# Rotary embedding on one core: each 2 MB slab as one stretch of DRAM, the cos and sin tables loaded in two halves

## The chip, the cores and the metric

The kernel runs on one core of a Trainium2 chip. The metric is device microseconds of one execution, median of the runs. The profile shows a second figure, the span: the time from the first to the last instruction that it recorded. In a run's own record the time is about 1.8 us above its span, for instance 165.31 us of time at a span of 163.5 us.

An execution more than 1.5% above the fastest of the same kernel counts as slow and is left out of every comparison; the others are fast.

The names in the profile: DVE is VectorE, ACT is ScalarE, POOL is GpSimd, PE is TensorE (PEld its weight loads), SP is SyncE; a q behind the name marks the issuing of DMA transfers. SBUF and PSUM are the two on-chip memories that hold the kernel's tiles, the blocks of 128 partitions (rows) that it names. A packet is one piece of a DMA transfer.

## The reference

```python
x:   [8, 2048, 8, 64] float32      # batch, position, head, d_head
cos, sin: [2048, 32] float32       # position, half of d_head

x1, x2 = x[..., :32], x[..., 32:]
out1 = x1 * cos - x2 * sin
out2 = x1 * sin + x2 * cos
out  = concatenate([out1, out2], axis=-1)
```

33.55 MB are read and 33.55 MB are written. The tables are 0.26 MB each.

## The kernel before

The 2048 positions of one batch are spread over 128 partitions, 16 neighbouring positions a partition: 32 KB of each partition's row. A slab is half of that, 8 positions a partition, 16 KB in each of 128 partitions, 2 MB. There are 16 slabs, first the eight batches with `l = 0`, then the eight with `l = 1`. Nine SBUF buffers hold slabs.

```python
    xv = x.rearrange("b (q r) h d -> b q (r h d)", q=P)
    ov = out.rearrange("b (q r) h d -> b q (r h d)", q=P)
    cos_src = cos.rearrange("(q r) d -> q r d", q=P)
    # ... sin_src alike
    cos_ps = tab_pool.tile([P, R, Dh], f32, tag="cp")      # PSUM, 128 x 512 fp32
    sin_ps = tab_pool.tile([P, R, Dh], f32, tag="sp")      # PSUM, 128 x 512 fp32
    # ... t1: PSUM, one buffer of 128 x 2048 fp32; o: PSUM, two of 128 x 512
    # ... t2: SBUF, three buffers

    def load(i):                                    # queue of SyncE
        b, l = slabs[i]
        xt = xpool.tile([P, SLAB], f32, tag="xt", name=f"xt{i}")
        for lo, n in spans(cuts(i)):                # slab 0 in two, the others whole
            nc.sync.dma_start(out=xt[:, lo : lo + n],
                              in_=xv[b, :, l * SLAB + lo : l * SLAB + lo + n])
            if i == 0 and lo == 0:
                nc.sync.dma_start(out=cos_sb, in_=cos_src)
                nc.sync.dma_start(out=sin_sb, in_=sin_src)
    for i in range(NBUF):                           # NBUF = 9
        load(i)

    # ... eye
    nc.scalar.mul(nsin, sin_sb, -1.0)
    nc.scalar.mul(neye, eye, -1.0)
    nc.vector.tensor_copy(cos_ps, cos_sb)
    nc.scalar.copy(sin_ps, sin_sb)
```

The arithmetic is mostly of kind "A": GpSimd writes x times sin into t2 in two instructions, VectorE multiplies x by cos from PSUM into t1, and then adds t1 and t2 back into the slab.

```python
            for u, tab in ((1, sin_sb), (0, nsin)):
                nc.gpsimd.tensor_mul(out=t2u[:, :, u, :]..., in0=xu[:, :, 1 - u, :]...,
                                     in1=rep(tab[:, r0 : r0 + nr, :], H))
        keep(nc.vector.tensor_mul(out=t1..., in0=xk, in1=rep(cos_ps[:, r0 : r0 + nr, :], 2 * H)))
        if kind == "A":
            keep(nc.vector.tensor_add(out=xt, in0=t1, in1=t2))
```

Slabs 5 and 10 use kinds "B" and "C": TensorE does the sum, and ScalarE copies it out of PSUM. ScalarE also issues the stores, two slabs behind, in its program order. So the stores of slab 3 and later stand behind ScalarE's copies for slab 5, and those of slab 8 and later behind its copies for slab 10. The load into a buffer waits for the store that empties it.

Of the kernel before, what the change touches and what calls it, by code (L numbers as in the profile page):

```python
# [10 lines left out]
def kernel(  # L11
# [7 lines left out]
    nc = tc.nc  # L19
# [6 lines left out]
    P = 128  # L26
# [3 lines left out]
    SL = 8  # L30
    n_half = R // SL
    SLAB = SL * HD
# [1 line left out]
    NBUF = 9  # L34
    C = 512

    xv = x.rearrange("b (q r) h d -> b q (r h d)", q=P)
    ov = out.rearrange("b (q r) h d -> b q (r h d)", q=P)
    cos_src = cos.rearrange("(q r) d -> q r d", q=P)
    sin_src = sin.rearrange("(q r) d -> q r d", q=P)  # L40

    const_pool = ctx.enter_context(tc.tile_pool(name="const", bufs=1))
    tab_pool = ctx.enter_context(tc.tile_pool(name="tab", bufs=1, space=PSUM))
# [6 lines left out]
    cos_sb = const_pool.tile([P, R, Dh], f32, tag="cb")  # L50
    sin_sb = const_pool.tile([P, R, Dh], f32, tag="sb")
    nsin = const_pool.tile([P, R, Dh], f32, tag="ns")
    eye = const_pool.tile([P, P], f32, tag="eye")
    neye = const_pool.tile([P, P], f32, tag="neye")
    cos_ps = tab_pool.tile([P, R, Dh], f32, tag="cp")
    sin_ps = tab_pool.tile([P, R, Dh], f32, tag="sp")
# [5 lines left out]
    def cuts(i):  # L62
        return [UNIT, UNIT] if i == 0 else [SLAB]
# [8 lines left out]
    def spans(sizes):  # L72
        lo = 0
        for n in sizes:
            yield lo, n
            lo += n

    def load(i):
        b, l = slabs[i]
        xt = xpool.tile([P, SLAB], f32, tag="xt", name=f"xt{i}")  # L80
        for lo, n in spans(cuts(i)):
            nc.sync.dma_start(
                out=xt[:, lo : lo + n],
                in_=xv[b, :, l * SLAB + lo : l * SLAB + lo + n],
            )
            if i == 0 and lo == 0:
                nc.sync.dma_start(out=cos_sb, in_=cos_src)
                nc.sync.dma_start(out=sin_sb, in_=sin_src)
        xts[i] = xt

    for i in range(NBUF):
        load(i)

    nc.gpsimd.memset(eye, 0.0)  # L94
    nc.gpsimd.affine_select(
        out=eye,
        in_=eye,
# [3 lines left out]
        pattern=[[-1, P]],  # L101
        channel_multiplier=1,
    )
    nc.scalar.mul(nsin, sin_sb, -1.0)  # L104
    nc.scalar.mul(neye, eye, -1.0)
    nc.vector.tensor_copy(cos_ps, cos_sb)  # L106
    nc.scalar.copy(sin_ps, sin_sb)  # L107

    def rep(a, n):
        return dataclasses.replace(a, ap=[a.ap[0][:], a.ap[1][:], [0, n], a.ap[-1][:]])  # L110
# [67 lines left out]
    def store(i, lo, n):  # L178
        b, l = slabs[i]
        keep(  # L180
            nc.scalar.dma_start(
                out=ov[b, :, l * SLAB + lo : l * SLAB + lo + n],
                in_=xts[i][:, lo : lo + n],
            )
        )

    for i in range(last + 1):
        if i == last:
            for k in range(i - LAG, i):
                store(k, 0, SLAB)  # L190
        for lo, n in spans(pieces(i)):
            rotate(i, lo, n)
            if i == last and lo == 0:
                store(i, 0, UNIT)
        if i == last:
            store(i, UNIT, UNIT)
        if LAG <= i < last:
            store(i - LAG, 0, SLAB)
        if i > LAG and i - LAG - 1 + NBUF <= last:
            load(i - LAG - 1 + NBUF)  # L200
# [30 lines left out]
```

## Time and profile before

| | before |
|---|---|
| time, median of 4 runs | 164.97 us |
| span of the profiled run | 163.5 us |
| VectorE busy / GpSimd busy | 142.8 / 138.8 us |
| DMA, two data queues, share of 16 engines' span | 49.8% + 48.6% |
| first multiply on VectorE | 6.90 us |
| first store issued | 19.25 us |

These are lines of the page's parts 2, 3 and 5. In part 2 a digit is the busy share of one fortieth of the span, in tenths. In part 5 the columns are line, engine, operation, tiles and shapes, count, then busy time and mean ns, then the idle time before and what ended most of it.

```profile
DVE  0439999999999999999999999999999999999900
POOL 1299999999999999699999999984999999995000
DMA  5999999999999999999999999999999999999995
...
q1 hardware_dynamic: 2736, 34.08, 49.8%
q10 hardware_dynamic: 2448, 33.56, 48.6%
...
L142 DVE TENSOR_TENSOR t<-xt,cos_ps 128x2048 f32<-128x2048 f32 (+1 forms) x34 | 73.5, 2168 | 1.0
...
L106 DVE COPY cos_ps<-cos_sb 128x512 f32<-128x512 f32 x1 | 0.7, 696 | 6.2 <-DMA cos_sb<-in_cos_dram 6.2
```

The DMA engines are full in every slice but the first and the last; 98.4% of 163.5 us is 160.9 us of work for each of the 16. VectorE (DVE) is almost as full. Two resources are thus near their limit. VectorE starts as soon as cos has been loaded and copied.

The timeline of the start, with start and length in us, engine, line and operation, and in brackets the idle time before it with its releaser:

```profile
6.17 0.70 DVE L106 COPY cos_ps<-cos_sb 128x512 f32<-128x512 f32 x1 [6.17 <-DMA cos_sb<-in_cos_dram]
...
6.90 1.23 DVE L142 TENSOR_TENSOR t<-xt,cos_ps 128x1024 f32<-128x1024 f32 x1
...
7.57 0.58 ACT L107 COPY sin_ps<-sin_sb 128x512 f32<-128x512 f32 x1
...
19.25 0.38 ACTq L181 DMA_DIRECT2D out_dram<-xt  x1
```

ScalarE's view (ACT) later on: after its last copy for slab 10 it issues the nine stores that are left.

```profile
121.02 0.59 ACT L156 COPY xt<-o 128x512 f32<-128x512 f32 x1 [1.13 <-PE o L155]
121.08 34.80 ACTq L181 DMA_DIRECT2D out_dram<-xt  x9
```

VectorE's last instruction of this run:

```profile
154.28 1.23 DVE L149 TENSOR_TENSOR xt<-t,t 128x1024 f32<-128x1024 f32 x1
```

In the trace's record of DMA packets a 16 KB packet took 611 ns in the median, for loads and for stores.

### The profile page before, as it was taken

What the parts mean: (1) busy time and instruction counts of PE and PEld (TensorE: products, weight loads), DVE (VectorE), ACT (ScalarE), POOL (GpSimd) and SP (SyncE); (2) the same over time, 40 slices, a digit from 0 to 9 for tenths busy, and PEclk for the clock granted to TensorE, in tenths of its full rate; (3) what the DMA queues carried; (4) which work ended last, traced back from release to release, by engine and by line L of the source; (5) the groups of instructions that cost most, each with busy time, mean ns of one, the idle gap of its engine ahead of it and who ended that gap; (6) DMA issues with size and microseconds to landing.
All of it is one profiled execution on the core that took longest, in us unless ns stands there. A gap on an engine that the chain in (4) does not pass through costs nothing. (4 is left out here: it accounts for less than half of the span.)

```text
span 163.5 us, 460 instructions
## 1 busy us (share of the span) xinstructions
PE 34.5 (21%) x64; PEld 13.8 (8%) x64; DVE 142.8 (87%) x67; ACT 12.0 (7%) x20; POOL 138.8 (85%) x70
## 2 busy tenths in 40 slices
PE   0000000000000049997000000699950000000000
PEld 0000000000000014442000000234410000000000
DVE  0439999999999999999999999999999999999900
ACT  3300000000000001233000000013320000000000
POOL 1299999999999999699999999984999999995000
PEclk9999999999999999999655555559996555555555
DMA  5999999999999999999999999999999999999995
GB/s 182 415 449 429 445 317 421 425 445 433 417 433 441 437 409 445 437 421 425 425 421 369 439 411 429 449 417 429 421 445 429 413 445 429 429 425 445 421 409 228
DMA packets 5186, 67.65 MB, mean 414 GB/s; under 512 B 576, under 2 KB 576, under 8 KB 832
## 3 DMA queue, kind: packets, MB, share of 16 engines
q1 hardware_dynamic: 2736, 34.08, 49.8%
q10 hardware_dynamic: 2448, 33.56, 48.6%
q14 instruction: 2, 0.02, 0.0%
HBM read 34.08 MB, written 33.55 MB: 414 GB/s over the span
## 5 line engine op out<-in xcount | busy, mean ns | idle before, releaser
L136 POOL TENSOR_TENSOR t<-xt,sin_sb 128x1024 f32<-128x1024 f32 (+1 forms) x32 | 70.4, 2201 | 10.3 <-DMA sin_sb<-in_sin_dram 5.6
L142 DVE TENSOR_TENSOR t<-xt,cos_ps 128x2048 f32<-128x2048 f32 (+1 forms) x34 | 73.5, 2168 | 1.0
L136 POOL TENSOR_TENSOR t<-xt,nsin 128x1024 f32<-128x1024 f32 (+1 forms) x32 | 70.4, 2202 | 0.0
L149 DVE TENSOR_TENSOR xt<-t,t 128x2048 f32<-128x2048 f32 (+1 forms) x30 | 64.5, 2150 | 5.6 <-POOL t L136 2.5
L170 PE MATMUL o<-t,eye 128*128 128x512 f32 x16 | 12.0, 843 | 86.3 <-DVE t L142 86.3
L174 ACT COPY xt<-o 128x512 f32<-128x512 f32 x8 | 4.7, 586 | 95.0 <-PE o L171 64.5
L170 PEld LDWEIGHTS o<-t,eye 128*128 128x128 f32 x16 | 3.9, 257 | 91.4 <-issue 91.4
L154 PE MATMUL o<-t,eye 128*128 128x512 f32 x16 | 8.2, 592 | 0.0
L155 PE MATMUL o<-t,eye 128*128 128x512 f32 x16 | 8.2, 592 | 0.0
L171 PE MATMUL o<-t,neye 128*128 128x512 f32 x8 | 6.9, 950 | 0.1
L106 DVE COPY cos_ps<-cos_sb 128x512 f32<-128x512 f32 x1 | 0.7, 696 | 6.2 <-DMA cos_sb<-in_cos_dram 6.2
L156 ACT COPY xt<-o 128x512 f32<-128x512 f32 x8 | 4.7, 586 | 9.0 <-PE o L155 9.0
L159 DVE TENSOR_TENSOR t<-xt,sin_ps 128x2048 f32<-128x2048 f32 x2 | 4.6, 2280 | 0.0
L171 PE MATMUL o<-t,eye 128*128 128x512 f32 x8 | 4.1, 592 | 0.0
L155 PEld LDWEIGHTS o<-t,eye 128*128 128x128 f32 x16 | 3.0, 190 | 3.8 <-issue 3.8
L154 PEld LDWEIGHTS o<-t,eye 128*128 128x128 f32 x16 | 3.0, 190 | 3.8 <-issue 3.8
L171 PEld LDWEIGHTS o<-t,neye 128*128 128x128 f32 x8 | 2.4, 324 | 5.3 <-DVE t L159 3.3
L171 PEld LDWEIGHTS o<-t,eye 128*128 128x128 f32 x8 | 1.5, 190 | 1.9 <-issue 1.9
L104 ACT ACT_TABLE_LOAD x1 | 1.3, 1283 | 0.7 <-PEq L215 0.7
L104 ACT ACTIVATE nsin<-sin_sb 128x512 f32<-128x512 f32 x1 | 0.6, 632 | 4.8 <-DMA sin_sb<-in_sin_dram 4.8
L107 ACT COPY sin_ps<-sin_sb 128x512 f32<-128x512 f32 x1 | 0.6, 578 | 0.0
L94 POOL MEMSET eye<- 128x128 f32 x1 | 0.2, 205 | 0.3 <-POOLq L215 0.3
(6 smaller groups left out, 1.0 us busy)
## 6 DMA issues: line engine op xcount, KB each, us to landing
xt<-in_x_dram SPq DMA_DIRECT2D x15, 2048.0 KB, 24.2
out_dram<-xt ACTq DMA_DIRECT2D x15, 2048.0 KB, 15.9
xt<-in_x_dram SPq DMA_DIRECT2D x2, 1024.0 KB, 6.0
out_dram<-xt ACTq DMA_DIRECT2D x2, 1024.0 KB, 8.3
cos_sb<-in_cos_dram SPq DMA_DIRECT2D x1, 256.0 KB, 5.0
sin_sb<-in_sin_dram SPq DMA_DIRECT2D x1, 256.0 KB, 5.2
```

Source lines behind the costliest of these rows:

```text
L104: nc.scalar.mul(nsin, sin_sb, -1.0)
L106: nc.vector.tensor_copy(cos_ps, cos_sb)
L136: nc.gpsimd.tensor_mul(out=t2u[:, :, u, :].rearrange("p (r h) d -> p r h d", h=H), in0=xu[:, :, 1 - u, :].rearrange("p (r h) d -> p r h d" ...
L142: nc.vector.tensor_mul(out=t1.rearrange("p (r k d) -> p r k d", r=nr, d=Dh), in0=xk, in1=rep(cos_ps[:, r0 : r0 + nr, :], 2 * H),)
L149: keep(nc.vector.tensor_add(out=xt, in0=t1, in1=t2))
L154: nc.tensor.matmul(o, eye, t1[:, cs], start=True, stop=False)
L155: nc.tensor.matmul(o, eye, t2[:, cs], start=False, stop=True)
L156: keep(nc.scalar.copy(xt[:, cs], o))
L159: nc.vector.tensor_mul(out=t2.rearrange("p (r k d) -> p r k d", r=nr, d=Dh), in0=xk, in1=rep(sin_ps[:, r0 : r0 + nr, :], 2 * H),)
L170: nc.tensor.matmul(o, eye, t1u[:, gs, u, :], start=True, stop=False)
L171: nc.tensor.matmul(o, eye if u else neye, t2u[:, gs, 1 - u, :], start=False, stop=True)
L174: keep(nc.scalar.copy(xu[:, gs, u, :], o.rearrange("p (g d) -> p g d", d=Dh)))
```

## The change

The intent: a slab becomes 1024 neighbouring positions, eight a partition, so that its 128 rows of 16 KB lie one behind the other in DRAM. The first eight slabs then need only the first half of the positions, so the tables are loaded in halves: the first where the whole tables were loaded before, the second behind slab 3. The copies are made in halves too. VectorE copies the first half of cos, ScalarE the second, so that VectorE does not have to wait for the second load in its own stream.

```diff
-    xv = x.rearrange("b (q r) h d -> b q (r h d)", q=P)
-    ov = out.rearrange("b (q r) h d -> b q (r h d)", q=P)
-    cos_src = cos.rearrange("(q r) d -> q r d", q=P)
-    sin_src = sin.rearrange("(q r) d -> q r d", q=P)
+    xv = x.rearrange("b (g q r) h d -> b g q (r h d)", q=P, r=SL)
+    ov = out.rearrange("b (g q r) h d -> b g q (r h d)", q=P, r=SL)
+    cos_src = cos.rearrange("(g q r) d -> g q r d", q=P, r=SL)
+    sin_src = sin.rearrange("(g q r) d -> g q r d", q=P, r=SL)
 ...
+    def tables(g):
+        gs = slice(g * SL, (g + 1) * SL)
+        nc.sync.dma_start(out=cos_sb[:, gs, :], in_=cos_src[g])
+        nc.sync.dma_start(out=sin_sb[:, gs, :], in_=sin_src[g])
 ...
-                in_=xv[b, :, l * SLAB + lo : l * SLAB + lo + n],
+                in_=xv[b, l, :, lo : lo + n],
             )
             if i == 0 and lo == 0:
-                nc.sync.dma_start(out=cos_sb, in_=cos_src)
-                nc.sync.dma_start(out=sin_sb, in_=sin_src)
+                tables(0)
 ...
     for i in range(NBUF):
         load(i)
+        if i == 3:
+            tables(1)
 ...
-    nc.scalar.mul(nsin, sin_sb, -1.0)
-    nc.scalar.mul(neye, eye, -1.0)
-    nc.vector.tensor_copy(cos_ps, cos_sb)
-    nc.scalar.copy(sin_ps, sin_sb)
+    for g in range(n_half):
+        gs = slice(g * SL, (g + 1) * SL)
+        nc.scalar.mul(nsin[:, gs, :], sin_sb[:, gs, :], -1.0)
+        if g == 0:
+            nc.vector.tensor_copy(cos_ps[:, gs, :], cos_sb[:, gs, :])
+            nc.scalar.mul(neye, eye, -1.0)
+        else:
+            nc.scalar.copy(cos_ps[:, gs, :], cos_sb[:, gs, :])
+        nc.scalar.copy(sin_ps[:, gs, :], sin_sb[:, gs, :])
 ...
-                out=ov[b, :, l * SLAB + lo : l * SLAB + lo + n],
+                out=ov[b, l, :, lo : lo + n],
```

The semaphore waits are not written in the kernel. The framework derives them, in program order.

## The prediction

> **What bounds it now.** The page shows the 16 DMA engines at 9 tenths in every slice but the first and last, 414 GB/s on average; the queues' packets add up to 98.4% of the span. In the packet records a 16 KB packet takes 611 ns in the median for loads and for stores, with a mean of 620 and 619.6 ns, so waiting on DRAM is worth at most 1.5%. VectorE is nearly as full (87%): after its first multiply at 6.90 us it runs to 155.5 us with one wait of note, 2.5 us on GpSimd.
>
> **The address pattern.** Packets stay 16 KB on both sides, and their median is also their floor, so a contiguous 2 MB stretch has next to nothing to win: under 1.3 us. The Trainium skill ("DMA: Bandwidth & Descriptors", Latency and other measured facts) reports lost rate only for pitches of 512 KiB and up; 32 KB here shows no loss, in agreement. I expect 611 ns again. The tables become 512 packets of 1 KB instead of 256 of 2 KB (84 ns): about 0.15 us.
>
> **The tables.** Half tables would land about 0.6 us sooner (0.26 MB less at 430 GB/s), alone nearly worthless with DMA the limit. But cos_ps is 128 x 512 fp32, 2 KB a partition, exactly one PSUM bank. Now ScalarE writes its second half while VectorE wants to read the first. The Trainium skill ("PSUM — Partial Sum Buffer", PSUM bank collisions raise a hardware error) says to guard by bank, not by address. No trace here shows it yet. I expect the generated dependencies to do that: the write stands earlier in the program, so VectorE's first multiply waits for ScalarE's copy of the second half, which waits for the second table load.
>
> That load stands in the queue behind slabs 0 to 3. Up to its end 8.9 MB must pass: by the windows 7.6 MB have passed at 20 us, at 430 GB/s the rest by 23.0. In the kernel before the tables were seen 0.8 us after their bytes had passed: 23.8. Two short ScalarE copies (half of 0.63 and 0.58 us, estimated) make 24.5. GpSimd starts near 6.3, fills its three t2 buffers and stops.
>
> VectorE then needs no wait for GpSimd, so slab 0 (four half-size instructions at 1.25, two at 2.35) is ready at 34.3 instead of 19.2: everything on VectorE moves by 15 us, and it ends near 170.6. The end: ScalarE holds the stores back until slab 10's PSUM copies are done (first store after them at 121.1 us before, 136.2 after); then nine stores, 16.8 MB, need 39 us at 430 GB/s plus 2 us to start: span about 177.3. Time is 1.4 us above span: 178.8 us. VectorE's own end plus one 1 MB store (4.7 us for 1 MB on an empty queue) gives 175.3, a little less.
>
> **Chances.** If the dependencies were by address, the time would be 163.5 to 165.5; I give that 11%.
>
> **What would show it.** The list of waits: VectorE's first table multiply waiting about 17 us for ScalarE's copy, itself waiting for the DMA of cos_sb or sin_sb; GpSimd waiting about 10 us for VectorE; first store at 34 us instead of 19; DMA tenths below 9 in a stretch before 136 us; VectorE busy time unchanged near 143 us; 16 KB packets still 611 ns. Right about the pattern but wrong about the bank: VectorE starts at about 6.3 us and the span is within 1%.
>
> **What would make it wrong.** Dependencies by address; the table loads placed earlier in the queue, each slab earlier being 4.9 us less; contiguous rows that slow the packets; a different order of stores that drains the backlog sooner or later.

## The result, and the profile after

| | before | after |
|---|---|---|
| time, median of 4 runs | 164.97 us | 180.48 us (180.26 to 180.87) |
| span of the profiled run | 163.5 us | 178.5 us |
| VectorE / GpSimd busy | 142.8 / 138.8 us | 142.5 / 138.7 us |
| first multiply on VectorE | 6.90 us | 24.92 us |
| first store issued | 19.25 us | 34.83 us |

The ratio is 1.0938, with a 95% interval of 1.0902 to 1.0973: slower. Ratios in this document are the mean time of one kernel's fast runs over that of the other's of the same rounds, so not quite the ratio of the medians that are quoted.

The same parts of the page as before:

```profile
DVE  0000039999999999999999999999999999999930
POOL 1496008999999999942999999999399999999000
DMA  5999999999999999930049999999999999999994
...
q1 hardware_dynamic: 3024, 34.08, 45.8%
q10 hardware_dynamic: 2448, 33.56, 44.5%
...
L153 DVE TENSOR_TENSOR t<-xt,cos_ps 128x2048 f32<-128x2048 f32 (+1 forms) x34 | 73.5, 2168 | 19.1 <-ACT cos_ps L117 18.2
...
L114 DVE COPY cos_ps<-cos_sb 128x256 f32<-128x256 f32 x1 | 0.4, 428 | 6.3 <-DMA cos_sb<-in_cos_dram 6.3
...
L117 ACT COPY cos_ps<-cos_sb 128x256 f32<-128x256 f32 x1 | 0.4, 376 | 17.0 <-DMA cos_sb<-in_cos_dram 17.0
```

The multiplies by cos still take 73.5 us, 2168 ns on average. What is new is the idle time before them: 18.2 us until ScalarE's copy (L117) of the second half of cos, a half that VectorE does not read before slab 8. That copy in turn waited 17.0 us for its load. The DMA queues' shares add up to 90.3% of 178.5 us, which is 161.2 us: the same work as the 160.9 us before, within 0.3 us. The DMA engines did not get slower. They got a hole, the `30049` in the row of tenths.

The timeline of VectorE's late start shows it instruction by instruction, and its last line is VectorE's last instruction:

```profile
6.28 0.43 DVE L114 COPY cos_ps<-cos_sb 128x256 f32<-128x256 f32 x1 [6.28 <-DMA cos_sb<-in_cos_dram]
...
13.83 2.31 POOL L147 TENSOR_TENSOR t<-xt,nsin 128x1024 f32<-128x1024 f32 x1
24.51 0.38 ACT L117 COPY cos_ps<-cos_sb 128x256 f32<-128x256 f32 x1 [17.05 <-DMA cos_sb<-in_cos_dram]
24.82 0.41 ACT L112 ACTIVATE nsin<-sin_sb 128x256 f32<-128x256 f32 x1
24.92 1.23 DVE L153 TENSOR_TENSOR t<-xt,cos_ps 128x1024 f32<-128x1024 f32 x1 [18.21 <-ACT cos_ps L117]
...
27.56 2.32 POOL L147 TENSOR_TENSOR t<-xt,sin_sb 128x1024 f32<-128x1024 f32 x1 [11.41 <-DVE xt L160]
...
34.83 9.79 ACTq L192 DMA_DIRECT2D out_dram<-xt  x2
...
169.85 1.22 DVE L160 TENSOR_TENSOR xt<-t,t 128x1024 f32<-128x1024 f32 x1
```

VectorE copied its half at 6.28 us and then did nothing until 24.92, the moment when ScalarE's copy ended (24.51 + 0.38 = 24.89). GpSimd, in contrast, read the first half of `nsin` at 13.83 us, long before ScalarE wrote the second half of the same SBUF tile at 24.82. So the halves of this SBUF tile are ordered by address, and those of the PSUM tile are not. GpSimd then stood still for 11.41 us with its three t2 buffers full.

After this one wait VectorE has none longer than 0.20 us, and it ends at 171.07 us, 146.2 us after its start. Before, it ended at 155.51, 148.6 us after its start; 2.5 us of those were a wait for GpSimd's first product, which is long finished in the kernel after. So a start 18.0 us later moves the end of VectorE's work by 15.6 us, and the span by 15.0.

During VectorE's wait at the start the DMA engines still run: the first nine slabs have free buffers to go to. Their hole comes later. Here are three windows of the kernel after; the columns are the window, its length, the busy time (with the number of instructions) of PE, PEld, DVE, ACT and POOL, the TensorE clock, and last the share of the DMA engines and GB/s:

```profile
6.70:24.90 18.20, 0.00 (x0) 0.00 (x0) 0.01 (x1) 1.16 (x5) 9.44 (x6) 1.00 1.02 431
...
76.00:91.00 15.00, 14.94 (x32) 5.99 (x30) 14.62 (x8) 4.10 (x7) 8.90 (x5) 1.00 0.09 39
...
174.00:178.50 4.50, 0.00 (x0) 0.00 (x0) 0.00 (x0) 0.00 (x0) 0.00 (x0) 0.50 0.50 211
```

From about 77 to 91 us all loads that have a buffer are done, and no store can be issued, because ScalarE is at its copies for slab 5 (or waits for them: 53.63 us before the first). VectorE works on through all of it, 14.62 us busy of 15:

```profile
79.13 0.59 ACT L185 COPY xt<-o 128x512 f32<-128x512 f32 x1 [53.63 <-PE o L182]
...
91.16 0.82 ACTq L192 DMA_DIRECT2D out_dram<-xt  x2
...
135.47 35.98 ACTq L192 DMA_DIRECT2D out_dram<-xt  x9
```

Before, the stores behind the same copies left at 76.7 us, before the loads had run out. The nine last stores leave at 135.47 us instead of 121.08.

### The profile page after: what moved, and what is told of

Read it like the earlier page. It is cut to its first block, busy times and chain, and to the rows that moved or that the text cites. A ratio compares the mean times of both kernels' runs of the same rounds, so it can differ in the third digit from the quotient of the medians.

```text
span 178.5 us, 465 instructions
## 1 busy us (share of the span) xinstructions
PE 32.3 (18%) x64; PEld 13.0 (7%) x64; DVE 142.5 (80%) x67; ACT 12.5 (7%) x23; POOL 138.7 (78%) x70
## 5 line engine op out<-in xcount | busy, mean ns | idle before, releaser
L153 DVE TENSOR_TENSOR t<-xt,cos_ps 128x2048 f32<-128x2048 f32 (+1 forms) x34 | 73.5, 2168 | 19.1 <-ACT cos_ps L117 18.2
L181 PE MATMUL o<-t,eye 128*128 128x512 f32 x16 | 10.3, 732 | 103.0 <-DVE t L153 103.0
L166 PE MATMUL o<-t,eye 128*128 128x512 f32 x16 | 8.2, 592 | 0.0
L165 PE MATMUL o<-t,eye 128*128 128x512 f32 x16 | 8.2, 592 | 0.0
L182 PE MATMUL o<-t,neye 128*128 128x512 f32 x8 | 6.2, 864 | 0.1
L182 PE MATMUL o<-t,eye 128*128 128x512 f32 x8 | 4.1, 592 | 0.0
L182 PEld LDWEIGHTS o<-t,neye 128*128 128x128 f32 x8 | 1.8, 250 | 4.2 <-DVE t L170 3.3
L117 ACT COPY cos_ps<-cos_sb 128x256 f32<-128x256 f32 x1 | 0.4, 376 | 17.0 <-DMA cos_sb<-in_cos_dram 17.0
L112 ACT ACTIVATE nsin<-sin_sb 128x256 f32<-128x256 f32 x2 | 0.8, 414 | 4.6 <-DMA sin_sb<-in_sin_dram 4.6
L118 ACT COPY sin_ps<-sin_sb 128x256 f32<-128x256 f32 x2 | 0.7, 364 | 0.0
```

Source lines behind the costliest of these rows:

```text
L112: nc.scalar.mul(nsin[:, gs, :], sin_sb[:, gs, :], -1.0)
L118: nc.scalar.copy(sin_ps[:, gs, :], sin_sb[:, gs, :])
L153: nc.vector.tensor_mul(out=t1.rearrange("p (r k d) -> p r k d", r=nr, d=Dh), in0=xk, in1=rep(cos_ps[:, r0 : r0 + nr, :], 2 * H),)
L165: nc.tensor.matmul(o, eye, t1[:, cs], start=True, stop=False)
L166: nc.tensor.matmul(o, eye, t2[:, cs], start=False, stop=True)
L181: nc.tensor.matmul(o, eye, t1u[:, gs, u, :], start=True, stop=False)
```

## The experiments

The theory: VectorE's first multiply waits for ScalarE's write to the other half of the same PSUM table; this moves all of VectorE's work by some 15 us, and with it the end. Rival 1: the contiguous rows slow the transfers. Rival 2: ScalarE, which waits for the second table load ahead of its stores, or its held stores later on, are what costs. All runs gave correct results. "Before" is the kernel before, run on the same chip in the same rounds.

### One PSUM bank for each half of the tables

```diff
-    cos_ps = tab_pool.tile([P, R, Dh], f32, tag="cp")
-    sin_ps = tab_pool.tile([P, R, Dh], f32, tag="sp")
+    tabs = [tab_pool.tile([P, 2, SL, Dh], f32, tag=f"tab{g}", ...) for g in range(n_half)]
+    cos_ps = [t[:, 0, :, :] for t in tabs]       # indexed by half from here on
+    sin_ps = [t[:, 1, :, :] for t in tabs]
```

> The changed kernel, but each half of the tables gets its own PSUM bank (cos and sin of one half together). Loads, addresses and ScalarE's instructions stay. Theory (VectorE waits because both halves of cos_ps lie in one PSUM bank): the first table multiply starts at 6.7 to 7.7 us instead of 24.9, the first store leaves near 26 us (ScalarE still waits for the second table load until 24.5), and the time is 163.5 to 166 us. Rival 1 (the contiguous rows slow the transfers): stays above 175 us. Rival 2 (ScalarE, blocked by the second table load, holds back the stores, and that is what costs): stays above 175 us.

Measured: 164.80 us against 165.06 us, ratio 0.997 (0.992 to 1.002). From its timeline:

```profile
7.09 0.36 ACT L122 COPY tab<-sin_sb 128x256 f32<-128x256 f32 x1
7.49 1.23 DVE L157 TENSOR_TENSOR t<-xt,tab 128x1024 f32<-128x1024 f32 x1 [0.82 <-ACT tab L122]
...
24.24 0.38 ACT L121 COPY tab<-cos_sb 128x256 f32<-128x256 f32 x1 [16.78 <-DMA cos_sb<-in_cos_dram]
...
24.66 0.38 ACTq L196 DMA_DIRECT2D out_dram<-xt  x1
```

The whole loss is gone, although addresses, loads and ScalarE's wait for the second table load are unchanged. Rival 1 falls. The part of rival 2 that blames ScalarE's early wait falls as well: the first store leaves at 24.66 us instead of 19.25, and no cost shows. VectorE still waits 0.82 us, now for ScalarE's write of sin into the tile it is about to read: the same kind of wait, shorter.

### The same two banks as one tile

```diff
+    tab = tab_pool.tile([P, n_half, 2, SL, Dh], f32, tag="tab")
+    cos_ps = [tab[:, g, 0, :, :] for g in range(n_half)]
+    sin_ps = [tab[:, g, 1, :, :] for g in range(n_half)]
```

> As e1_bank_per_half, but the two banks belong to one tile. Theory (dependencies by bank): VectorE starts at 6.7 to 7.7 us, time 163.5 to 166.5 us. Rival (dependencies by whole PSUM tile): VectorE starts near 24.9 us, time about 180.

Measured: 181.62 us (one run, state unknown). Its timeline:

```profile
24.83 0.36 ACT L119 COPY tab<-sin_sb 128x256 f32<-128x256 f32 x1
25.23 1.23 DVE L154 TENSOR_TENSOR t<-xt,tab 128x1024 f32<-128x1024 f32 x1 [18.54 <-ACT tab L119]
```

This went against the theory as it was expected to turn out. The second half lies in another bank here (a half is 512 fp32 columns, 2 KB a partition; that a bank has this size is the prediction's figure, and no run shows where one ends), and VectorE waits for it all the same: it starts at 25.23 us, right after ScalarE's last write to the tile ended at 25.19. So the framework ordered this PSUM tile as a whole, not by pieces of 2 KB. In the changed kernel each table is a tile of just 2 KB a partition, and the two readings could not be told apart. One run of unknown state is enough for this, as the two readings are 18 us apart in VectorE's start. What helped in the run before was that the halves became two tiles.

### The addresses alone

The kernel before with `xv`, `ov` and the loads of the change; the tables stay in one load and one copy each (`"(g q r) d -> q g r d"`, two rows of 1 KB a partition).

> The kernel before with contiguous 2 MB slabs alone; tables still in one load each (two rows of 1 KB a partition) and one copy each. Theory: 16 KB packets at a median of 611 ns, time within 0.7% of before, 164 to 166 us. Rival 1 (contiguous rows slow the transfers): above 170 us. Hope of the change (contiguous rows are faster): under 163.5 us.

Measured: 165.86 us against 165.06 us, ratio 1.0043 (0.9977 to 1.011): same. Its data queues:

```profile
q1 hardware_dynamic: 2992, 34.08, 49.9%
q10 hardware_dynamic: 2448, 33.56, 48.2%
```

That is 98.1% of a span of 163.7 us, 160.6 us of DMA work, as before. The 16 KB packets have a median of 611 ns in both directions. The main idea of the change has no effect that these runs can tell from none (the interval goes from 0.2% faster to 1.1% slower).

### The split alone

The changed kernel with the four views of before (`cos_src[:, gs, :]` in place of `cos_src[g]`, `xv[b, :, l * SLAB + lo : ...]` in place of `xv[b, l, :, ...]`).

> The changed kernel with the addresses of before: tables in two halves alone. Theory: VectorE starts near 24.9 us, time 179.5 to 181.5 us as the changed kernel. Rival 1 (addresses): 164 to 166 us.

Measured: 180.30 us against 165.06 us, ratio 1.0919 (1.0861 to 1.0977). From its list of waits (engine, tile and line, releaser: us in total, times, longest):

```profile
DVE t L153 <- ACT cos_ps L117: 18.7, 1, 18.7
ACT cos_ps L117 <- DMA cos_sb<-in_cos_dram: 16.9, 1, 16.9
```

The split alone gives the whole loss, with the same wait.

### The second load earlier or later

`if i == 3: tables(1)` becomes `i == 1` or `i == 5`, which moves the load by two slabs, 4.19 MB.

> The changed kernel with the second table load issued after slab 1 instead of slab 3, 4.19 MB earlier in the queue. At 430 GB/s that is 9.75 us: VectorE starts near 15.2 us, its end and the time move by the same amount: about 171 us (169.5 to 172). If the wait is not what costs, the time stays at 180.

> The changed kernel with the second table load issued after slab 5, 4.19 MB later: VectorE starts near 34.7 us and the time is about 190 us (188.5 to 191.5). If the wait is not what costs, the time stays at 180.

Measured: 170.79 us (ratio 1.0339, 1.0306 to 1.0372) and 190.11 us (ratio 1.1528, 1.1476 to 1.158); before had 165.12 us in these rounds (the median of seven, one of them slow, 169.72 us, and not in the ratios). The first multiply's group, with its first and last start in us, first for the earlier load:

```profile
L153 DVE TENSOR_TENSOR t<-xt,cos_ps x34: 1229/2296/2296, 15.0 to 158.6; 128x2048 f32<-128x2048 f32 x30, 128x1024 f32<-128x1024 f32 x4
```

and for the later one:

```profile
L153 DVE TENSOR_TENSOR t<-xt,cos_ps x34: 1228/2296/2296, 34.5 to 178.1; 128x2048 f32<-128x2048 f32 x30, 128x1024 f32<-128x1024 f32 x4
```

The spans are 168.6, 178.5 and 188.2 us for first multiplies at 15.0, 24.9 and 34.5 us: 153.6 us between start and end in all three, within 0.1 us. In this range each microsecond of wait costs one microsecond. Taken backwards, a start later than about 9.9 us (163.5 less 153.6, an estimate that no run tried) is what begins to cost. The kernel before starts 3.0 us earlier than that, and 2.5 us of these go into VectorE's wait for GpSimd.

### The copy of the second half where it is needed

```diff
+    def spread(g):
+        gs = slice(g * SL, (g + 1) * SL)
+        nc.scalar.mul(nsin[:, gs, :], sin_sb[:, gs, :], -1.0)
+        if g == 0:
+            nc.scalar.mul(neye, eye, -1.0)
+        keep(nc.vector.tensor_copy(cos_ps[:, gs, :], cos_sb[:, gs, :]))
+        nc.scalar.copy(sin_ps[:, gs, :], sin_sb[:, gs, :])
+    spread(0)                     # in place of the loop over both halves
 ...
     for i in range(last + 1):
+        if i == B:                # slab 8
+            spread(1)
```

> The changed kernel, the tables still in one PSUM bank each, but the copies of the second half stand in the program where slab 8, the first that needs them, begins, and VectorE makes the copy of cos itself. Theory (an ordering by bank, in program order): VectorE starts at 6.7 to 7.5 us and pays about 0.4 us for the copy at slab 8; time 163.5 to 166 us. Rival (two halves in one bank cost in any order): above 170 us.

Measured: 165.05 us against 165.12 us, ratio 0.9994 (0.9964 to 1.0025). From VectorE's timeline, the copy just before slab 8:

```profile
82.20 0.42 DVE L115 COPY cos_ps<-cos_sb 128x256 f32<-128x256 f32 x1
82.65 2.30 DVE L153 TENSOR_TENSOR t<-xt,cos_ps 128x2048 f32<-128x2048 f32 x1
```

And from its list of waits:

```profile
ACT sin_ps L116 <- DVE t L170: 30.3, 1, 30.3
```

One PSUM tile for both halves of a table costs nothing that shows when the program order is right. The wait shows the same ordering the other way round: ScalarE's write to the second half of `sin_ps` waited 30.3 us for VectorE's read of the first half. (This copy is not kept in program order: the framework placed it ahead of ScalarE's copies for slab 5, at 61.34 us.) No harm shows: the first copy for slab 5 starts at 63.48 us, against 63.58 in the kernel before.

### cos read from SBUF

VectorE's multiply reads `cos_sb`; the copies of cos to PSUM are taken out.

> The changed kernel, VectorE's multiply reading cos from its SBUF tile, with no copy to PSUM. The SBUF tiles of GpSimd were seen to be ordered by address. Theory (only a tile in PSUM is ordered as a whole): VectorE's first multiply starts near 6.3 us although the second half of the same SBUF tile lands near 24 us. Rival (any tile that VectorE reads is ordered as a whole): it starts near 24.5 us. What the time does is open: VectorE then reads two SBUF operands beside GpSimd.

Measured: 218.65 us (one run, state unknown). From its timeline:

```profile
6.56 1.23 DVE L149 TENSOR_TENSOR t<-xt,cos_sb 128x1024 f32<-128x1024 f32 x1 [6.56 <-DMA cos_sb<-in_cos_dram]
```

And from its groups, kept apart by shape, the same multiply with count, busy time and mean ns:

```profile
L149 DVE TENSOR_TENSOR t<-xt,cos_sb 128x2048 f32<-128x2048 f32 x30 | 121.3, 4047 | 0.8
```

The multiply starts at 6.56 us, so for VectorE too this SBUF tile is ordered by address; of the tiles tried, only those in PSUM were ordered whole. The time is far worse for another reason: the 128x2048 multiply takes 4047 ns, against 2295 ns in the median with cos in PSUM. The Trainium skill, "SBUF — State Buffer", Who interferes with whom, says that a VectorE instruction with two SBUF inputs contends with a GpSimd instruction that reads SBUF. This run agrees. The same half-size multiply took 3.30 us beside GpSimd and 1.23 us at the end, when GpSimd had stopped at 209.08 us, so it is not the reading from SBUF by itself that is slow:

```profile
12.61 3.30 DVE L149 TENSOR_TENSOR t<-xt,cos_sb 128x1024 f32<-128x1024 f32 x1
...
209.34 1.23 DVE L149 TENSOR_TENSOR t<-xt,cos_sb 128x1024 f32<-128x1024 f32 x1
```

That is a good reason for the table of cos to be in PSUM.

### The stores one slab sooner

`LAG = 2` becomes `LAG = 1` in the changed kernel, so that slabs 3 and 8 are stored before ScalarE's copies hold the rest. The loads that refill the buffers also stand one slab sooner in the program.

> The changed kernel with every store placed one slab sooner in ScalarE's order, so that slabs 3 and 8 leave before ScalarE's copies of slabs 5 and 10 hold the rest. VectorE still starts near 24.9 us and ends near 171 us. Theory (VectorE's late start sets the end; the 14 us in which the DMA engines idle are its consequence): the idle stretch shrinks to some 5 us, the span is VectorE's end plus 5 us or so, the time 177 to 179 us. Rival (the held stores and full buffers are what costs): time falls to 166 to 172 us.

Measured: 178.08 us (the median of four with one slow run; the three fast ones lie between 177.82 and 178.12) against 165.64 us, ratio of fast runs 1.0756 (1.0723 to 1.0788).

> The kernel of e9_stores_one_slab_sooner once more, because its profile fell in the slow state while its other runs did not (177.8 to 178.1 us). For a fast trace: VectorE starts near 24.8 us and ends near 171 us, the DMA engines idle some 5 us near 80 us instead of 14, the span is near 176 us.

Measured: 177.85 us, span 176.1 us, one run, at the clock and span of the fast runs. Its page:

```profile
DVE  0000039999999999999999999999999999999970
...
DMA  6999999999999999999809999999992999999945
```

VectorE starts at 24.7 us and its last store leaves at 170.9 us, as in the changed kernel. The hole in the DMA row has shrunk: from 83 to 94 us the windows show a share of 0.54, which is 5.1 us idle, against 0.30 from 74 to 94 us in the changed kernel, 14.0 us idle. A second hole has appeared instead, with a share of 0.62 from 128 to 138 us, 3.8 us idle, and the engines idle more towards the end. Moving the stores gave back 2.4 us of the span's 15 (3.1 us if each kernel is set against before in its own rounds), though it left part of the held stores and of the hole in place. That the rest does not belong to them is shown by VectorE: it has no wait above 0.2 us after its start in either run, so neither hole delays it, and it ends at 170.9 us here. The span ends 5.2 us after that, against 7.4 us in the changed kernel. So the held stores cost what lies behind VectorE's end, some 2 to 3 us, and the rest of rival 2 falls. They are held in the kernel before as well, and there the loads had not run out.

### Both repairs

One bank for each half and `LAG = 1` together, as the best version in sight.

> e1_bank_per_half with the same sooner stores, as the best version that the runs point to. The DMA engines are already busy to the end there, so I expect no more than 0.5% from it: 164 to 165.5 us.

Measured: 165.01 us against 165.64 us, ratio 0.9964 (0.9931 to 0.9996). With the wait removed the DMA engines are full until the last slice, and moving the stores has nothing to fill. No version tried beats the kernel before by more than half a per cent.

## Why the prediction was right

The prediction said 178.8 us, between 175.5 and 181.5; measured were 180.48 us.

- **The address pattern.** Predicted without effect, packets at 611 ns. The addresses alone gave a ratio of 1.0043 with an interval that holds 1, and 611 ns. Right.
- **The wait.** Predicted: VectorE's first multiply waits some 17 us for ScalarE's copy of the second half and starts at 24.5 us. Measured: 18.2 us, start at 24.92. Two small errors partly cancel in this: the load was seen at 24.51 us and not at 23.8, and VectorE had to wait for one ScalarE copy of 0.38 us and not for two of 0.6 together. Giving each half its own tile removed the loss, the split alone reproduced it, and moving the load moved it microsecond for microsecond.
- **The reason for the wait.** The prediction said that the ordering goes by PSUM bank, and named the Trainium skill, "PSUM — Partial Sum Buffer", PSUM bank collisions raise a hardware error. This step was wrong. The one-tile run showed that the ordering goes by the whole tile, 4 KB a partition there: VectorE waited for a write to the other 2 KB and started at 25.23 us. That the wait came out right all the same is partly luck, as the table of the changed kernel is one tile and, by the prediction's figure, one bank; the repair would have been misjudged, for spreading one tile over two banks does not help. Why the framework does it this way, no run shows. Whether the hardware needs the order within one bank, as that section says, was not tried either.
- **GpSimd.** About 10 us of waiting for VectorE were predicted; the long one was 11.41 us.
- **The first store.** Predicted at 34.3 us, measured at 34.83.
- **The end.** The prediction had two ways to the end, the held stores (177.3 us) and VectorE's end with one more store (175.3), and took the later. That choice was right: with the stores moved, the span fell to 176.1 us, set by VectorE's end. The last nine stores were predicted at 136.2 us, measured at 135.47. From there the prediction took 41 us to the end of the span; it was 43.0. The mis-sized term is the end of it: the window from 174 us shows the DMA engines half busy over 4.5 us, so the last 2.2 us of the span carry no data, and the sum had left them out. The prediction also set the time 1.4 us above the span, by taking the median time and the profiled run's span from different runs; in one and the same run it is 1.8 us. In sum: 0.7 us too much up to the stores, 1.9 us too little behind them, 0.5 us too little above the span (180.48 less 178.5 is 2.0, the prediction added 1.5), which makes the 1.7 us that were missing.
- **What was not foreseen.** The prediction expected the DMA engines below 9 tenths "in a stretch before 136 us" without saying why or how long: it was an almost empty 15 us at 76 to 91 us, made by nine full buffers and by stores held behind ScalarE's copies. Moving the stores gave back 2.4 us of it, as the run above shows.

## What to carry to other kernels

When a table is filled in pieces and read in pieces, look at what the generated waits are attached to, not only at which bytes are touched: here a PSUM tile was ordered as a whole, over all of its 4 KB a partition, while the SBUF tiles were ordered by address. Give each piece its own tile, or place its write in the program just before its first reader. And a load issued for later must not stand in front of anything needed now: its place in the queue (here 8.9 MB deep, 24 us) becomes the wait of whatever is ordered behind it, even though the DMA engines are busy all that time.

## What the Trainium skill lacked or had wrong

- "PSUM — Partial Sum Buffer", PSUM bank collisions raise a hardware error, advises to guard by bank, or bank and quadrant, and says that the compiler back end adds dependencies at that grain. No page was found that says at what grain the framework of this kernel orders PSUM accesses. It was the whole tile: with one tile of 4 KB a partition VectorE started at 25.23 us, 0.04 us after ScalarE's last write into the other 2 KB; with two tiles at 7.49 us.
- "DMA: Bandwidth & Descriptors", Latency and other measured facts, gives rates for row pitches from 512 KiB up. For the pitches of 32 KB and 16 KB (contiguous), the page has nothing; both gave 611 ns for a 16 KB packet, 26.8 GB/s for each engine.
- "SBUF — State Buffer", Who interferes with whom, names the contention of a VectorE instruction with two SBUF inputs but gives no measured duration for `tensor_tensor`. Beside a busy GpSimd a 128x2048 multiply took 4047 ns on average, against 2295 ns with one input in PSUM. GpSimd lost as well: its 128x1024 multiply by sin took 4315 ns, against 2337 ns in the changed kernel.
